# A sliding-window attention block in float16 pairs: other slots in the first three blocks and the last, and 24 low halves made by GpSimd

## The chip, the cores and the metric

One core of a Trainium2 chip runs the whole kernel. The metric is the device time of one execution in microseconds (us); the time before is the median of three runs, 1381.35 us (1379.68 to 1383.4). The engines are named as in the profile: PE (TensorE, with PEld for its weight loads), DVE (VectorE), ACT (ScalarE), POOL (GpSimd) and SP (SyncE, which issues most transfers). Each runs its own instructions in one fixed order and waits on semaphores for the others.

## The reference, cut to what matters

Of the reference's trunk only one layer runs (DEPTH is 1): 4096 tokens, 1024 channels, 16 query heads on 4 key heads, a window of 128 keys, a bias by distance, and one learned sink for each head.

```python
xn = rms_norm(x, norm_g[layer])
q, k, v, z = jnp.split(xn @ w_in, [nq, nq + nkv, nq + 2 * nkv], axis=-1)
o = banded_attention(q_heads(q, B, T), kv_heads(k, B, T), kv_heads(v, B, T),
                     t5_table, SWA_WINDOW, sinks)
y = (merge_heads(o, B, T) * jax.nn.silu(z)) @ w_out
x = x + y
return rms_norm(x, final_g)
```

## The kernel before, in words

**Number format.** Every large operand is held as two float16 tiles: a high half, the value rounded (made by ACT), and a low half, the rest (value minus high half, made by DVE, in `split`, `sum_to` and the functions that return a `low`). A product is three passes: high by high, high by low, low by high.

**Blocks.** The 4096 tokens are worked in 16 blocks of 256 (`block`, the index is `tb`). In each, q, z (the gate) and the output projection o are products of 2 by 2 blocks of the weights with 2 by 2 blocks of the tokens. From block 2 on for q and block 3 on for z and o, they are made with seven products in place of eight, which need sums and differences of the weights' blocks (`LEFT` and `RIGHT` name them: 11, s1 to s4, t1 to t4 ...). Before that (`PLAIN`), and for o in the last block, eight plain products are used. PE time of one product is 48 matmuls for q and z and 12 longer ones for o.

**Preparing the weights.** z's plain weights are split by `plain_z` in four steps, one for each of the blocks 11, 12, 21, 22, in the slots `ZBLOCKS`; block 22 is split by POOL. o's are split by `plain_o` in `OBLOCKS`. The sums are made by `sums`, in chunks of a quarter of the rows (c = 0 to 3), in the slots `SUMS` for q, z and o: one load of 1 MB into the tile `stage` (of which there is one, so that a chunk can only be loaded when the one before is done), a scaling by ACT (L225), four sums or differences by POOL (L187), and for each of the four a split in `sum_to`: high half by ACT (L237), low half by DVE (L239), and a store to DRAM, which is issued from ACT's queue one slot later. The weights are then streamed back from DRAM by SP: `load_s` (L344) into the four `ws` buffers, `load_q` (L361) and `load_fifth` (L356).

**What sets the order.** Each block's steps stand in slots, 25 to a block (`STEADY`, `FIRST`, `NEXT_TO_LAST`, `LAST`); inside a slot in the order of `PHASES`. A step is put there with `at`, or with `at_split` as two parts: high in the phase "high", low in the phase "low". Attention is done in four pairs a block (two groups of heads by two tiles of 128 tokens; `Pair`): scores on PE, `post` and `normalise` on DVE, `exps` on ACT, `turn` (transposes on PE, high half on ACT, low half and mask on DVE: L631, L632), `values` on PE, `gate` on DVE. The slots of the eleven steps come from "pairs"; `PAIRS_BY` moves those of the first three blocks, `SHORT` is the pattern of a pair in the last block. In the slots from `STATIC` = 90 on, PE, ACT, DVE and POOL keep the program's order as it is written. In slots 20 to 89 the builder chooses every engine's order itself from the priorities and its own estimate of times, and in slots 0 to 19 that of all engines but PE. SP's order is always the builder's.

```python
    ZBLOCKS = (6, 7, 9, 11)
    SUMS = {"q": (16, 20, 26, 33), "z": (39, 48, 51, 58), "o": (62, 71, 76, 81)}
    w = work.tile([P, 2, 512], F16, tag="wsp", name="wsp", bufs=3)
    SHORT = (0, 1, 2, 3, 5, 2, 3, 4, 5, 7, 8, 9)
    with tc.manual_schedule(engines={mybir.EngineType.PE}):
        emit(range(20))
    emit(range(20, STATIC))
    with tc.manual_schedule(engines=ENGINES):
        emit(range(STATIC, total))
```

Of the kernel before, what the change touches and what calls it, by code (L numbers as in the profile page):

```python
# [21 lines left out]
P = 128  # L22
# [36 lines left out]
def tile_swa_block(ctx, tc, x, xt, t5, norm_g, final_g, w_q, w_kv, w_z, sinks, w_out, hot, out):  # L59
# [80 lines left out]
    ZBLOCKS = (6, 7, 9, 11)  # L140
    OBLOCKS = (18, 20, 25, 28)
    PAIRS_BY = {0: (1, 4, 2, 3), 1: (2, 2, 2, 2), 2: (0, 1, 0, 2)}
    QSUMS_IN, FIFTH_IN, SPREAD_IN, XLOAD = 7, 9, 5, 7
    SUMS = {"q": (16, 20, 26, 33), "z": (39, 48, 51, 58), "o": (62, 71, 76, 81)}
# [90 lines left out]
    def sum_to(s, where, c, f, scale):  # L235
        w = work.tile([P, 2, 512], F16, tag="wsp", name="wsp", bufs=3)
        nc.scalar.activation(w[:, 0], f, AF.Copy, scale=scale)  # L237
        at("turn", s + 1, lambda: store(where, w, c))
        return lambda: nc.vector.scalar_tensor_tensor(w[:, 1], f, scale, w[:, 0], op0=OP.mult, op1=OP.subtract)  # L239

    def sum_q(s, n, name, c, f):
        return sum_to(s, wqs[n], c, f, 1.0)

    def sum_z(s, n, name, c, f):
        return sum_to(s, wzs[name], c, f, 1.0)
# [303 lines left out]
    class Pair:  # L549


        def __init__(self, tb, gp, t):
            self.tb, self.gp, self.t = tb, gp, t
            self.first = tb == 0 and t == 0
            self.s, self.pt, self.pm, self.c = {}, {}, {}, None

# [20 lines left out]
        def post(self, e):  # L577

            g = 2 * self.gp + e
# [25 lines left out]
        def exps(self, e):  # L605

            for u in range(4 * e, 4 * e + 4):
# [4 lines left out]
        def normalise(self, e):  # L612
            rl = work.tile([P, 4], F32, tag="rl", name="rl", bufs=3)
            nc.vector.reciprocal(rl, self.l[:, 4 * e:4 * e + 4])
            cu = self.c[:, 4 * e:4 * e + 4, :P]
            nc.vector.tensor_tensor(cu, cu, rl[:, :, None].to_broadcast([P, 4, P]), op=OP.mult)  # L616

        def turn(self, e):

            p = ps("tp", 2)  # L620
# [61 lines left out]
    def split_y(tb, name):  # L682

        s = Y[(tb, *YSUM[name][0])] if name in YSUM else Y[tb, int(name[0]) - 1, int(name[1]) - 1]
        YO[name] = work.tile([P, 2, 512], F16, tag="op", name="yo", bufs=4)
        yo = YO[name]
# [3 lines left out]
    def product_o(left, right, p, fresh):  # L690
        k = 0
        for c in range(4):
            for wi, yi in PASSES:
                nc.tensor.matmul(p, YO[left][:, yi, c * P:(c + 1) * P], right(c, wi), start=fresh and k == 0,  # L694
# [163 lines left out]
    SHORT = (0, 1, 2, 3, 5, 2, 3, 4, 5, 7, 8, 9)  # L858

    def moved(pairs, by):  # L860
# [14 lines left out]
    def block(tb):  # L875
# [48 lines left out]
        if isplain["o"]:  # L924
# [3 lines left out]
            for b, s in S["yplain"].items():  # L928
                at_split(s, split_y, tb, b)
            plain(slots, ("o", tb), "bacb" if last else "cbac" if tb + 1 < PLAIN["z"] else "cabc",  # L930
                  lambda i, j, k, p, fresh: product_o(f"{i}{k}", stream(("o", 4 * i + 2 * j + k - 7), f"{k}{j}"), p,
# [160 lines left out]
```

## Time and profile before

| what | before |
|---|---|
| time, median of three runs | 1381.35 us (1379.68 to 1383.4) |
| the profiled execution's own time | 1378.16 us |
| its span, first to last instruction | 1376.4 us |
| PE busy | 1337.0 us, 97% |
| DVE busy | 1199.3 us, 87% |
| ACT busy | 798.6 us, 58% |
| POOL busy | 443.8 us, 32% |

The profile is of one execution. Times are in us from the first instruction, unless marked ns; L239 is line 239 of the kernel. A busy time is the time in which at least one instruction of the engine ran. In brackets behind an instruction stands how long its engine was idle before it, and what ended that.

### The profile page before, as it was taken

The page shows a single profiled execution, that of the slowest core. Times are in us where ns is not written, and L with a number is a line of the kernel's source. Part 1 is how long each engine was busy: PE and PEld are TensorE (multiplying, and loading weights), DVE is VectorE, ACT ScalarE, POOL GpSimd, SP SyncE. Part 2 cuts the span into 40 slices and gives each one's busy share as a digit, 9 for nine tenths or more (in the row PEclk, how much of TensorE's full clock was granted, in tenths as well). Part 3 has the DMA queues.
Part 4 walks back from the last instruction along what each step waited for, and adds up shares of the span by engine and source line. Part 5 has one row for each costly group of instructions (what it writes and reads, how often), then busy time and mean ns, then how long its engine had stood idle before and what let it go on. Part 6 is the DMA issues. An engine that isn't in the chain of part 4 may idle for free.

```text
span 1376.4 us, 39292 instructions
## 1 busy us (share of the span) xinstructions
PE 1337.0 (97%) x16246; PEld 1083.8 (79%) x16246; DVE 1199.3 (87%) x2719; ACT 798.6 (58%) x2052; POOL 443.8 (32%) x406
## 2 busy tenths in 40 slices
PE   5899999999999999999999999999999999999987
PEld 4898678697796978879787887978879687887953
DVE  6989888978889899897989989898898989989895
ACT  6777665655555555555566556556555556655552
POOL 1612432525224143232414224241422424232121
PEclk9999999999999999999999999999999999999999
DMA  9996996889977694866859487694957769495566
GB/s 356 328 374 223 352 390 227 342 321 355 346 276 294 211 342 169 319 242 236 322 184 340 182 301 266 228 340 157 336 213 274 267 230 344 150 335 211 209 236 260
DMA packets 75603, 381.65 MB, mean 277 GB/s; under 512 B 9472, under 2 KB 10784, under 8 KB 42912
## 3 DMA queue, kind: packets, MB, share of 16 engines
q1 hardware_dynamic: 64352, 358.12, 70.6%
q10 hardware_dynamic: 11072, 21.02, 4.1%
q8 instruction: 127, 2.08, 0.6%
q14 instruction: 52, 0.43, 0.1%
HBM read 340.05 MB, written 39.06 MB: 275 GB/s over the span
## 4 chain that ended last, share of the span: by engine, by line
PE 78%; DVE 11%; ACT 4%; issue 3%; DMA 2%; POOL 0%; ACTq 0%; SPq 0%; POOLq 0%; DVEq 0%
PE pa L375 16%; PE pb L375 15%; PE pc L694 11%; PE o L651 6%; PE pa L694 5%; PE s L574 5%; PE pc L375 5%; PE pc L473 5%; PE pb L394 5%; PE tp L624 3%; PE pb L694 3%; DVE wsp L239 2%; DVE c L601 1%; DVE q L427 1%; DVE pt L631 1%
## 5 line engine op out<-in xcount | busy, mean ns | idle before, releaser
L375 PEld LDWEIGHTS <-ws 128*128 128x128 f16 x7008 | 399.3, 98 | 28.2 <-issue 15.9
L694 PEld LDWEIGHTS <-yo 128*128 128x128 f16 x1392 | 134.2, 98 | 144.4 <-issue 2.3
L375 PEld LDWEIGHTS <-wq 128*128 128x128 f16 x3984 | 226.8, 98 | 9.8 <-issue 5.8
L609 ACT ACTIVATE c<-c,m 128x129 f32<-128x129 f32 x512 | 198.9, 391 | 31.8 <-DVE m L601 31.2
L694 PE MATMUL pc<-ws,yo 128*128 128x512 f16 x744 | 170.4, 379 | 0.1
L601 DVE CUSTOM_DVE_ANT_0 c<-s,bias,sink 128x128 f32<-128x128 f32 x496 | 153.2, 349 | 7.8 <-DVE s L592 0.5
L284 POOL TENSOR_TENSOR rr<-ms,mhalf 128x1 f32<-128x1 f32 x62 | 35.6, 582 | 333.6 <-DVE ms L282 267.0
L616 DVE TENSOR_TENSOR c<-c,rl 128x512 f32<-128x512 f32 x128 | 128.0, 1002 | 3.8
L631 DVE SCALAR_TENSOR_TENSOR pt<-tp,pt 128x512 f16<-128x512 f32 x128 | 87.1, 683 | 36.0 <-ACT pt L628 35.9
L574 PE MATMUL s<-K,q 128*128 128x192 f16 x1024 | 107.8, 247 | 3.6 <-DVE m L601 3.3
L688 DVE TENSOR_TENSOR yo<-y,yo 128x512 f16<-128x512 f32 x100 | 82.3, 823 | 33.2 <-ACT yo L687 33.2
L375 PE MATMUL pb<-xs,ws 128*128 128x128 f16 x1872 | 111.2, 219 | 0.0
L322 POOL TENSOR_TENSOR xf<-xf 128x512 f32<-128x512 f32 x56 | 83.9, 1507 | 81.3 <-DVE xb L311 70.5
L404 ACT ACTIVATE mc<-pa 128x512 f32<-128x512 f32 x67 | 39.9, 595 | 117.0 <-PE pa L375 78.3
L404 ACT ACTIVATE mc<-pb 128x512 f32<-128x512 f32 x53 | 31.6, 597 | 129.7 <-PE pb L375 97.0
L375 PE MATMUL pb<-xb,ws 128*128 128x128 f16 x1776 | 106.4, 219 | 0.0
L187 POOL TENSOR_TENSOR wst<-wst 128x512 f32<-128x512 f32 x48 | 71.4, 1497 | 91.2 <-ACT wst L225 49.8
L632 DVE TENSOR_TENSOR pm<-pt,own_m 128x1024 f16<-128x1024 f16 x128 | 96.8, 758 | 3.7
L628 ACT ACTIVATE pt<-tp 128x512 f16<-128x512 f32 x128 | 74.1, 593 | 44.0 <-PE tp L624 39.9
L574 PEld LDWEIGHTS <-q 128*128 128x128 f16 x1024 | 85.9, 98 | 16.7 <-DVE m L601 5.6
L680 POOL TENSOR_TENSOR y<-y,y 128x512 f32<-128x512 f32 x48 | 75.4, 1570 | 68.2 <-DVE y L658 48.8
L609 ACT ACTIVATION_READ_ACCUMULATOR c<-c,m 128x1 f32 x512 | 96.4, 188 | 0.0
(135 smaller groups left out, 2677.6 us busy)
## 6 DMA issues: line engine op xcount, KB each, us to landing
ws<-wos SPq DMA_DIRECT2D x68, 1024.0 KB, 6.0
ws<-wzss SPq DMA_DIRECT2D x52, 1024.0 KB, 6.2
ws<-wost SPq DMA_DIRECT2D x48, 1024.0 KB, 5.5
ws<-wzs SPq DMA_DIRECT2D x47, 1024.0 KB, 5.5
ws<-wqs SPq DMA_DIRECT2D x31, 1024.0 KB, 5.1
xin<-in_x SPq DMA_DIRECT2D x34, 512.0 KB, 4.4
xf<-in_xt SPq DMA_DIRECT2D x32, 512.0 KB, 4.5
r<-in_x SPq DMA_DIRECT2D x30, 512.0 KB, 6.0
```

Source lines behind the costliest of these rows:

```text
L322: nc.gpsimd.tensor_tensor(dst, l, r, op=OP.subtract)
L375: nc.tensor.matmul(place(p, c), left(kc, wi)[:, c * P:(c + 1) * P], right_x(tb, right, kc, xi), start=fresh and c == 0 and k == 0, stop=c ...
L574: nc.tensor.matmul(s[:, hp, 0:3 * HD], lhs, rhs, start=hl == 0, stop=hl == 1)
L601: nc.vector.tensor_tensor_reduce(out=cu, in0=sv, in1=b, scale=-1.0 / SCORE, scalar=sink[:, g, r, hp:hp + 1], op0=OP.add, op1=OP.min, accum ...
L609: nc.scalar.activation(cu, cu, AF.Exp, bias=self.m[:, u:u + 1], scale=-1.0, accum_out=self.l[:, u:u + 1])
L616: nc.vector.tensor_tensor(cu, cu, rl[:, :, None].to_broadcast([P, 4, P]), op=OP.mult)
L631: nc.vector.scalar_tensor_tensor(w[:, 1], p, SP, w[:, 0], op0=OP.mult, op1=OP.subtract)
L632: nc.vector.tensor_tensor(m.rearrange("p l (h q) -> p (l h) q", h=4), w.rearrange("p l (h q) -> p (l h) q", h=4), own_m[:, None, :].to_bro ...
L651: nc.tensor.matmul(o[e * HD:(e + 1) * HD, :], v[:, vt, vi, g * HD:(g + 1) * HD], w[e][:, pi], start=k == 0, stop=k == n - 1)
L680: nc.gpsimd.tensor_tensor(Y[(tb, *dst)], Y[(tb, *l)], Y[(tb, *r)], op=op)
L688: return lambda: nc.vector.tensor_tensor(yo[:, 1], s, yo[:, 0], op=OP.subtract)
L694: nc.tensor.matmul(p, YO[left][:, yi, c * P:(c + 1) * P], right(c, wi), start=fresh and k == 0, stop=k == 11, skip_group_check=not fresh)
```

## The change

- The low halves of q's sums in all four chunks and of z's in chunks 0 and 1 (16 + 8 = 24 of 48) are made by POOL as a plain difference, not by DVE as a scaled one (the scale is 1.0); their store is issued one slot later.
- Other numbers for `ZBLOCKS`, `OBLOCKS`, `PAIRS_BY`, `QSUMS_IN`, `FIFTH_IN`, `SPREAD_IN` (which nothing uses), `XLOAD` and `SUMS`.
- In the last block other slots for the pairs (`SHORT`), for v's differences (`vd`, `dv`), for three steps of z, for the eight products of o and for three of the splits of y. `yo` is kept under a name with the block in it.
- A branch that would scale the probabilities on ACT is added; it is taken for blocks under `SCALED_ON_ACT`, which is 0. `step` is a test while the program is built.

```diff
-    ZBLOCKS = (6, 7, 9, 11)
-    OBLOCKS = (18, 20, 25, 28)
-    PAIRS_BY = {0: (1, 4, 2, 3), 1: (2, 2, 2, 2), 2: (0, 1, 0, 2)}
-    QSUMS_IN, FIFTH_IN, SPREAD_IN, XLOAD = 7, 9, 5, 7
-    SUMS = {"q": (16, 20, 26, 33), "z": (39, 48, 51, 58), "o": (62, 71, 76, 81)}
+    SCALED_ON_ACT = 0
+    LOW_ON_POOL = 6
+    ZBLOCKS = (7, 9, 2, 3)
+    OBLOCKS = (16, 16, 24, 33)
+    PAIRS_BY = {0: (1, 4, 2, 3), 1: (2, 2, 2, 1), 2: (3, 1, 0, 2)}
+    QSUMS_IN, FIFTH_IN, SPREAD_IN, XLOAD = 5, 12, 8, 6
+    SUMS = {"q": (14, 19, 25, 38), "z": (41, 52, 53, 55), "o": (60, 69, 73, 76)}
...
-    def sum_to(s, where, c, f, scale):
+    def sum_to(s, where, c, f, scale, pool=False):
         w = work.tile([P, 2, 512], F16, tag="wsp", name="wsp", bufs=3)
         nc.scalar.activation(w[:, 0], f, AF.Copy, scale=scale)
-        at("turn", s + 1, lambda: store(where, w, c))
+        at("turn", s + (2 if pool else 1), lambda: store(where, w, c))
+        if pool:
+            return lambda: nc.gpsimd.tensor_tensor(w[:, 1], f, w[:, 0], op=OP.subtract)
         return lambda: nc.vector.scalar_tensor_tensor(w[:, 1], f, scale, w[:, 0], op0=OP.mult, op1=OP.subtract)
 
     def sum_q(s, n, name, c, f):
-        return sum_to(s, wqs[n], c, f, 1.0)
+        return sum_to(s, wqs[n], c, f, 1.0, c < LOW_ON_POOL)
 
     def sum_z(s, n, name, c, f):
-        return sum_to(s, wzs[name], c, f, 1.0)
+        return sum_to(s, wzs[name], c, f, 1.0, c + 4 < LOW_ON_POOL)
...
         def normalise(self, e):
+            self.step(e, 2)
             rl = work.tile([P, 4], F32, tag="rl", name="rl", bufs=3)
             nc.vector.reciprocal(rl, self.l[:, 4 * e:4 * e + 4])
+            if self.tb < SCALED_ON_ACT:
...
-        YO[name] = work.tile([P, 2, 512], F16, tag="op", name="yo", bufs=4)
-        yo = YO[name]
+        YO[tb, name] = work.tile([P, 2, 512], F16, tag="op", name="yo", bufs=4)
+        yo = YO[tb, name]
...
-    SHORT = (0, 1, 2, 3, 5, 2, 3, 4, 5, 7, 8, 9)
+    SHORT = (1, 2, 2, 4, 6, 2, 3, 3, 5, 7, 8, 9)
...
-    LAST = dict(STEADY, vd=13, dv=15, zs12=18, zp22=19, zs22=20,
-                pairs={p: tuple(s + d for d in SHORT) for p, s in zip(STEADY["pairs"], (11, 14, 17, 20))},
-                oplain=(24, 27, 26, 28, 29, 32, 30, 33), yplain={"11": 21, "12": 24, "21": 27, "22": 30}, res=25)
+    LAST_PAIRS = (11, 14, 17, 20)
+    LAST_V, LAST_DV, LAST_Z12, LAST_ZP, LAST_Z22 = 17, 18, 19, 21, 23
+    LAST_O = (24, 30, 26, 30, 34, 35, 31, 35)
+    LAST_Y = (21, 24, 27, 29)
+    LAST = dict(STEADY, vd=LAST_V, dv=LAST_DV, zs12=LAST_Z12, zp22=LAST_ZP, zs22=LAST_Z22,
+                pairs={p: tuple(s + d for d in SHORT) for p, s in zip(STEADY["pairs"], LAST_PAIRS)},
+                oplain=LAST_O, yplain=dict(zip(BLOCKS, LAST_Y)), res=25)
```

## Rows read from the trace of the kernel before

**Rows 1.** Page, part 1: busy us, share of the span and instructions.

```profile
PE 1337.0 (97%) x16246; PEld 1083.8 (79%) x16246; DVE 1199.3 (87%) x2719; ACT 798.6 (58%) x2052; POOL 443.8 (32%) x406
```

**Rows 2.** Windows: length; busy PE, PEld, DVE, ACT, POOL; PE's granted clock; DMA share, GB/s.

```profile
50.00:62.00 12.00, 7.57 (x82) 7.16 (x80) 11.51 (x18) 7.03 (x11) 10.15 (x9) 0.72 0.84 272
62.00:230.00 168.00, 162.36 (x2167) 139.45 (x2164) 147.38 (x373) 110.55 (x279) 50.35 (x47) 1.00 0.83 313
...
400.00:725.00 325.00, 325.00 (x3996) 265.82 (x3994) 290.72 (x653) 187.13 (x498) 104.56 (x96) 1.00 0.72 260
...
1290.00:1335.00 45.00, 40.95 (x466) 30.89 (x464) 38.72 (x111) 25.70 (x80) 12.56 (x12) 1.00 0.72 257
...
54.45:61.25 6.80, 5.50 (x48) 5.43 (x49) 6.64 (x8) 2.09 (x4) 6.80 (x6) 0.50 0.76 263
```

**Rows 3.** Waits of PE, 62 to 400 us: total, times, longest.

```profile
PE o L651 <- DVE pt L631: 3.9, 4, 2.3
PE s L574 <- DVE m L601: 2.9, 5, 1.1
PE o L651 <- DVE pm L632: 1.5, 2, 1.2
```

**Rows 4.** Instructions of PE in order of time, at the waits of the first blocks.

```profile
53.24 0.79 PE L375 MATMUL pa<-xb,ws 128*128 128x128 f16 x11 [2.71 <-DVE q L427]
55.75 4.13 PE L375 MATMUL pa<-xb,ws 128*128 128x128 f16 x37 [1.72 <-DVE ws L163]
...
144.30 0.38 PE L651 MATMUL o<-pt,v 128*64 128x512 f16 x1 [2.31 <-DVE pt L631]
...
232.44 0.38 PE L651 MATMUL o<-pt,v 128*64 128x512 f16 x1 [0.86 <-DVE pt L631]
...
333.57 0.51 PE L574 MATMUL s<-K,q 128*128 128x192 f16 x4 [1.14 <-DVE m L601]
```

**Rows 5.** Low halves of sums on DVE, 62 to 236 us: by line.

```profile
L239 DVE SCALAR_TENSOR_TENSOR wsp<-wst,wsp 128x512 f16<-128x512 f32 x23 | 22.4, 983 | 0.5 <-ACT wsp L237 0.5
```

**Rows 6.** Durations by line, whole span: count, ns min/median/max, first and last start.

```profile
L168 POOL TENSOR_TENSOR ws<-wst,ws x4: 1149/1602/1608, 43.5 to 57.8; 128x512 f16<-128x512 f32 x4
L239 DVE SCALAR_TENSOR_TENSOR wsp<-wst,wsp x48: 661/688/1780, 59.8 to 362.5; 128x512 f16<-128x512 f32 x48
L631 DVE SCALAR_TENSOR_TENSOR pt<-tp,pt x128: 652/683/692, 88.1 to 1351.8; 128x512 f16<-128x512 f32 x128
```

**Rows 7.** The normalisations on DVE, 62 to 230 us: count, busy, mean ns.

```profile
L616 DVE TENSOR_TENSOR c<-c,rl 128x512 f32<-128x512 f32 x16 | 12.1, 764 | 0.1
```

**Rows 8.** DVE's instructions of z's weights, in order of time.

```profile
54.64 3.74 DVE L163 SCALAR_TENSOR_TENSOR ws<-wst,gs,ws 128x512 f16<-128x512 f32 x3
```

**Rows 9.** The last block in order of time, DVE and PE.

```profile
1312.60 0.29 DVE L592 COPY_PREDICATED s<-sel,s 128x128 f32<-128x128 int32 x1
...
1314.46 2.08 DVE L514 SCALAR_TENSOR_TENSOR z<-z,cc 128x512 f32<-128x512 f32 x2
...
1316.46 0.68 DVE L631 SCALAR_TENSOR_TENSOR pt<-tp,pt 128x512 f16<-128x512 f32 x1
...
1352.17 2.75 PE L694 MATMUL pb<-ws,yo 128*128 128x512 f16 x12
...
1352.50 0.69 DVE L632 TENSOR_TENSOR pm<-pt,own_m 128x1024 f16<-128x1024 f16 x1
```

**Rows 10.** Waits of PE, 1290 us to the end: total, times, longest.

```profile
PE o L651 <- DVE pt L631: 2.7, 2, 1.8
PE o L651 <- DVE pm L632: 0.9, 2, 0.5
```

**Rows 11.** q's summed weights: the reloads, and PE's first product on them.

```profile
170.47 3.42 SPq L361 DMA_DIRECT2D wq<-wqs x2
...
184.31 2.84 PE L375 MATMUL pb<-xs,wq 128*128 128x128 f16 x48
```

**Rows 12.** The two reloads of rows 11: time to landing.

```profile
DMA to landing us min/median/max: 8.1/8.2/8.3
```

More of the change, by code (lines that the diff above doesn't have):

```diff
@@ L555, in __init__, with step @@
             self.s, self.pt, self.pm, self.c = {}, {}, {}, None
+            self.steps = [0, 0]
+        def step(self, e, n):
+            assert self.steps[e] == n, (self.tb, self.gp, self.t, e, n)
+            self.steps[e] = n + 1
         def scores(self, e):
@@ L577, in post @@
         def post(self, e):
+            self.step(e, 0)
             g = 2 * self.gp + e
@@ L605, in exps @@
         def exps(self, e):
+            self.step(e, 1)
             for u in range(4 * e, 4 * e + 4):
@@ L612, in normalise @@
         def normalise(self, e):
+            self.step(e, 2)
             rl = work.tile([P, 4], F32, tag="rl", name="rl", bufs=3)
             nc.vector.reciprocal(rl, self.l[:, 4 * e:4 * e + 4])
+            if self.tb < SCALED_ON_ACT:
+                for u in range(4):
+                    cu = self.c[:, 4 * e + u, :P]
+                    nc.scalar.activation(cu, cu, AF.Copy, scale=rl[:, u:u + 1])
+                return
             cu = self.c[:, 4 * e:4 * e + 4, :P]
@@ L618, in turn @@
         def turn(self, e):
+            self.step(e, 3)
             p = ps("tp", 2)
@@ L684, in split_y, with product_o @@
         s = Y[(tb, *YSUM[name][0])] if name in YSUM else Y[tb, int(name[0]) - 1, int(name[1]) - 1]
-        YO[name] = work.tile([P, 2, 512], F16, tag="op", name="yo", bufs=4)
-        yo = YO[name]
+        YO[tb, name] = work.tile([P, 2, 512], F16, tag="op", name="yo", bufs=4)
+        yo = YO[tb, name]
         nc.scalar.activation(yo[:, 0], s, AF.Copy)
         return lambda: nc.vector.tensor_tensor(yo[:, 1], s, yo[:, 0], op=OP.subtract)
-    def product_o(left, right, p, fresh):
+    def product_o(tb, left, right, p, fresh):
         k = 0
@@ L693, in product_o @@
             for wi, yi in PASSES:
-                nc.tensor.matmul(p, YO[left][:, yi, c * P:(c + 1) * P], right(c, wi), start=fresh and k == 0,
+                nc.tensor.matmul(p, YO[tb, left][:, yi, c * P:(c + 1) * P], right(c, wi), start=fresh and k == 0,
                                  stop=k == 11, skip_group_check=not fresh)
@@ L930, in block @@
             plain(slots, ("o", tb), "bacb" if last else "cbac" if tb + 1 < PLAIN["z"] else "cabc",
-                  lambda i, j, k, p, fresh: product_o(f"{i}{k}", stream(("o", 4 * i + 2 * j + k - 7), f"{k}{j}"), p,
+                  lambda i, j, k, p, fresh: product_o(tb, f"{i}{k}", stream(("o", 4 * i + 2 * j + k - 7), f"{k}{j}"), p,
                                                       fresh),
@@ L947, in block @@
                      lambda p: add_p(tb, 1, 0, p)]
-            chain(S["o"], ("o", tb), "cab", lambda n, p: product_o(LEFT[n], stream("o", RIGHT[n]), p, n in (0, 1, 3)),
+            chain(S["o"], ("o", tb), "cab", lambda n, p: product_o(tb, LEFT[n], stream("o", RIGHT[n]), p, n in (0, 1, 3)),
                   steps, False)
```

## The prediction, made before the change was run

> **What bounds the kernel now.** I began with busy times by engine: PE is busy for 97% of the span [rows 1], so what can be won without taking products away is what PE waits. Where that is, the windows show [rows 2]: in the 325 us from 400 us on PE is busy in every microsecond, and the code's count for a steady block (14 products of 48 matmuls, 7 of 12, and some 240 others, together about 998) says that the 3996 matmuls there are four blocks, so a block is 81.25 us and a slot 3.25 us. The change touches nothing that runs there but what is left over from the start. PE has idle time in the first three blocks and in the last: 4.4 of 12 us from 50 to 62 us, 5.6 of 168 us from 62 to 230 us, 4.1 of 45 us from 1290 to 1335 us. Next I asked who ends these waits. From 62 to 400 us all three large ones end with DVE, 8.3 us together [rows 3]; in the last block two do, 3.6 us [rows 10]. DVE is busy for 147 of the 168 us, GpSimd for 50 [rows 2]. So the kernel is bound by PE, and in the stretches that are changed by DVE's order: PE stands while DVE does something less urgent first. At 144.30 PE waits 2.31 us and at 232.44 again 0.86 us for the low half of the probabilities (L631) [rows 4]; L239 and the splits of o's weights stand among DVE's work there.
>
> **Part 1: 24 low halves to GpSimd.** In the stretch that matters DVE makes 23 of them in 22.4 us, 0.98 us each [rows 5]; the 24th is the first, at 59.8 us [rows 6]. DVE loses 22.4 + 0.98 = 23.4 us of work. On GpSimd the same difference with the same shape and types is L168, 1.60 us by the median [rows 6]; 24 of them are 38.4 us, which brings GpSimd from 50 to about 89 of 168 us, 53%. It stays off the path as long as the store a slot later is not missed.
>
> What this costs DVE again must be bounded. L239 takes 0.69 us by the median and up to 1.78 us, while L631, whose source lies in PSUM, never takes over 0.69 [rows 6]. So beside GpSimd's work an instruction with two SBUF sources can take 1.09 us more and one with a PSUM source nothing. If each subtraction met one such instruction, DVE would lose 24 x 1.09 = 26.2 us, more than it is given. The lower end is the normalisations in this very stretch, whose mean is 0.764 us [rows 7], 0.08 above L239's median of the same size, although GpSimd was busy for 50 us: 16 x 0.08 = 1.2 us. I take the lower end, since it is measured where the subtractions will lie, so that DVE gains some 22 us in this stretch.
>
> The Trainium skill has a rule against this part (SBUF — State Buffer, section on the two separate sides): GpSimd and a VectorE instruction with two SBUF inputs lock the pair of ports they share for a whole instruction, and the other stands still. By that rule alone the full 38.4 us would be lost where DVE has such an instruction ready. The trace shows it for the lengthened L239, and shows as well that L631 is not touched.
>
> What is it worth to PE? The waits at 144.30 and 232.44 go, 3.2 us. Of the other 5.1 us of [rows 3] I take a third, 1.7 us: one of them, 1.14 us at 333.57 [rows 4], lies beside sums of o, which stay on DVE, and the rest behind other work of DVE. **Minus 4.9 us**; the ends are 0 and minus 8.3.
>
> Queues: the stores are issued by ACT and wait for GpSimd, and behind them stand ACT's exponentials and high halves of the probabilities; one extra slot is 3.25 us, two subtractions. On GpSimd the square root for x's norm (L284) and x's own sums (L322) stand behind the subtractions. The rival for slower has the price.
>
> **Part 2: other slots up to 89.** ZBLOCKS now asks for block 21 first, then 22, then 11 and 12, but PE begins with 11. At 55.75 PE waits 1.72 us for the low half of the last quarter of 11 [rows 4], the first of three such instructions that took 3.74 us [rows 8]. With that of 21 ahead of it the wait grows by a third of that, **plus 1.25 us**. The wait of 2.71 us before (for a q evacuation on DVE) I leave as it is, and also the clock, which was granted at half (1.2 of 2.4 GHz) from 54.45 to 61.25 us [rows 2]: it fell after the first of the two waits, while PE stood in the second. Bounds: both waits and the half clock go (rival 2), or 2.5 us more. The other slots (SUMS, OBLOCKS, PAIRS_BY, QSUMS_IN, FIFTH_IN, XLOAD) I cost at nothing: the order is the builder's there, the chunks of sums follow one another through the single stage buffer, and each transfer lands while PE has products of other matrices to do. If that cover is gone, rival 3 gives the price.
>
> **Part 3: the last block**, where the order is as written. At slot 19 the first pair's values wait 1.79 us for L631 and 0.45 for the mask; at slot 22 the second pair's wait the rest of the 3.6 us [rows 10]. Before the L631 at 1316.46 stand, in slot 18, the post of the third pair's first half, from 1312.60 to 1314.46 = 1.86 us, and the last of two z steps, half of 2.08 us [rows 9]. SHORT moves that post to slot 19 and zs12 moves to 19: 2.9 us less ahead of it. The normalisation that comes one slot later returns up to 0.7 us. So about 0.2 us of this wait is left. For the second pair the same post (of the fourth pair) leaves slot 21, and z's step in 20 goes to 23: its wait goes too. Against this, the last pair's values now have one product of o between the transposes and them where they had two: the mask ran from 1352.50 to 1353.19 while the first of those products had ended by 1352.17, when the second began [rows 9]; that is 0.7 us to wait, with PE's first six matmuls as a small cover. Sum: -3.6 + 0.2 + 0.7 = **minus 2.7 us**; ends 0 and -3.6. The products of o that move behind the values are the same in number, and the tail of additions, norm and stores behind the last product is unchanged. The weights for the last two have three products in between, about 7.8 us by the length in [rows 9] less overlap, to land. The key `YO[tb, name]`, `step` and the branch under SCALED_ON_ACT issue nothing.
>
> **Sum.** -4.9 + 1.25 - 2.7 = -6.35 us. The profiled execution took 1378.16 us, 3.19 us below the median, so 1371.8 us by its own time, and 1375.0 us against the median of 1381.35. A measurement of this kernel can tell about 0.3% from no change, 4.1 us.
>
> **Rivals.**
> 1. *DVE is given nothing.* Every subtraction meets an instruction with two SBUF sources: 26.2 us lost for 23.4 won. The lengthened L239 speaks for it, the normalisations' mean against it. PE's waits of [rows 3] stay: 1378.16 + 1.25 - 2.7 = 1376.7, or 1379.9 us against the median. This is also what would come out if the builder's order hardly followed the new slots. The skill's rule of the port pair leads here.
> 2. *The opening's waits go.* With block 21 and the POOLED block 22 out of the way early, DVE reaches q's evacuation and 11 in time: 2.71 + 1.72 us and half of the 6.8 us of half clock, 3.4 us, go, and the 1.25 is not paid: 1371.8 - 9.1 = 1362.7, or 1365.9 us. For it: DVE had 11.5 of 12 us of work there [rows 2]. Against it: the last quarter of z's raw weights arrives late whatever the order is.
> 3. *Slower: q's summed weights come late.* The reload of the first starts at 170.47 us and takes 8.2 us [rows 11, 12], so it lands at 178.7, and PE uses it at 184.31: 5.6 us of slack. The fourth chunk's slot goes from 33 to 38; if its load really moved by the 5 slots, 16.25 us, PE would stand for 10.6 us in block 2, with nothing behind it to do in order. With half of part 1's gain: 1378.16 + 10.6 + 1.25 - 2.7 - 2.45 = 1384.9, or 1388.1 us. It decides from a delay of 5.6 us on, and makes the kernel slower by 0.3% from about 13.6 us. Against it: chunks follow the stage buffer more than their slot.
>
> **How the numbers follow.** The forecast has 0.45, rival 1 0.18, rival 2 0.2, rival 3 0.17. The forecast's own range, 1370 to 1380, has about a tenth of its weight over 1377.2, where it can't be told from no change. Faster by over 0.3%: 0.4 + 0.2 = 0.6; within: 0.18 + 0.05 = 0.23; slower: 0.17. The range for 8 in 10 goes from 1363, at which rival 2 has a little more than it asks, to 1387, short of rival 3's full price.
>
> **What would show it.** Right: L239 only 24 times, 24 subtractions of about 1.6 us on GpSimd, DVE's busy time from 62 to 230 us down by some 20 us; no wait of PE over 1 us behind L631 before 250 us; PE idle from 1290 to 1335 us about 1.5 us in place of 4.1. Wrong: normalisations or masks at 1.5 us by the mean (rival 1); full clock from 50 to 62 us (rival 2); PE waiting for DMA or idle before the first product on the reloaded weights (rival 3); or an idle time in the last block that only moved from the first pairs to the last.

## The result, and the profile after

| what | before | after |
|---|---|---|
| time, median | 1381.76 us (1379.37 to 1383.4) | 1391.66 us (1388.89 to 1393.79), six runs |
| ratio, 95% interval | | 1.0079 [1.0068, 1.0089] |
| span of the profiled execution | 1376.4 us | 1389.2 us |
| mean clock granted to PE | 0.996 | 0.989 |

The change makes the kernel slower, by about 10 us by the medians and 12.8 us by the two profiled spans. The forecast was 1375.0, its range 1363 to 1387: wrong in sign, and outside the range. The lines of the code have moved by 2 to 19: what was L239 (DVE's low half of a sum) is L243, GpSimd's new one is L242; L163 is L165, L173 L175 (load of a chunk), L187 L189, L344 L348, L375 L379, L574 L584, L601 L612, L616 L634, L631 L650, L632 L651, L651 L670, L688 L707, L694 L713.

Part 1 of the page after, in the columns of [rows 1]:

```profile
PE 1342.9 (97%) x16246; PEld 1086.9 (78%) x16246; DVE 1192.8 (86%) x2695; ACT 799.4 (58%) x2052; POOL 464.9 (33%) x430
```

PE has the same 16246 matmuls but is busy for 5.9 us longer, and its idle time, span less busy, is 46.3 us where it was 39.4. These two, 5.9 + 6.9, are the whole 12.8 us. DVE is busy for 6.5 us less over the span, and that has bought nothing. The windows say where, in the columns of [rows 2]:

```profile
50.00:62.00 12.00, 6.01 (x73) 5.69 (x71) 10.01 (x15) 8.48 (x13) 8.71 (x9) 0.75 0.98 319
62.00:230.00 168.00, 159.23 (x2061) 134.48 (x2060) 136.04 (x336) 104.92 (x259) 71.84 (x66) 0.98 0.82 311
230.00:400.00 170.00, 161.99 (x1878) 126.59 (x1876) 136.26 (x314) 89.69 (x231) 61.77 (x52) 0.96 0.82 309
...
1303.00:1348.00 45.00, 43.21 (x512) 33.84 (x510) 39.41 (x114) 27.16 (x84) 12.10 (x12) 1.00 0.76 270
...
400.00:1303.00 903.00, 903.00 (x11096) 738.72 (x11095) 808.57 (x1808) 519.67 (x1379) 290.87 (x267) 1.00 0.72 258
```

The window of the kernel before that [rows 2] does not show:

```profile
230.00:400.00 170.00, 166.35 (x1945) 130.70 (x1943) 143.29 (x329) 94.58 (x234) 64.50 (x52) 1.00 0.87 331
```

PE idles for 6.0 us in the first stretch (4.4 before), 8.8 in the second (5.6 before) and 8.0 in the third (3.7 before). The steady blocks have no idle time, as before. The last block, which now comes 13 us later, idles for 1.8 us where [rows 2] gives 4.1: that part did what its sum forecast. The clock column is the other half of the loss: 0.98 and 0.96 where it was 1.00. Waits of PE from 62 to 400 us, to be laid beside [rows 3]:

```profile
PE s L584 <- DVE m L612: 6.6, 1, 6.6
PE pb L713 <- DMA ws<-wos: 3.6, 1, 3.6
PE pa L713 <- DMA ws<-wos: 2.4, 1, 2.4
PE o L670 <- DVE pm L651: 2.0, 1, 2.0
```

The many waits of before have made room for four large ones. Behind a low half of the probabilities (3.9 us in four waits of [rows 3]) PE now waits for 0.2 us. So the waits that the prediction wanted gone are gone, and larger ones stand at other places. Those rows of PE, in order of time:

```profile
53.97 0.77 PE L379 MATMUL pa<-xb,ws 128*128 128x128 f16 x11 [2.58 <-ACT ws L164]
58.15 4.13 PE L379 MATMUL pa<-xb,ws 128*128 128x128 f16 x37 [3.41 <-DVE ws L165]
...
160.88 0.82 PE L584 MATMUL s<-K,q 128*128 128x192 f16 x4 [6.62 <-DVE m L612]
...
265.34 5.28 PE L713 MATMUL pb<-ws,yo 128*128 128x512 f16 x12 [3.60 <-DMA ws<-wos]
...
335.45 1.01 PE L670 MATMUL o<-pm,dv 128*64 128x512 f16 x5 [1.99 <-DVE pm L651]
...
355.34 4.27 PE L713 MATMUL pa<-ws,yo 128*128 128x512 f16 x12 [2.42 <-DMA ws<-wos]
```

**The longest, 6.62 us.** Scores wait until DVE has read the ones before them (L612). DVE's row of work ahead of that, in order of time:

```profile
152.31 2.52 DVE L707 TENSOR_TENSOR yo<-y,yo 128x512 f16<-128x512 f32 x2
154.76 0.17 DVE L627 RECIPROCAL rl<-l 128x4 f32<-128x4 f32 x1
154.96 1.55 DVE L634 TENSOR_TENSOR c<-c,rl 128x512 f32<-128x512 f32 x1
156.44 1.75 DVE L707 TENSOR_TENSOR yo<-y,yo 128x512 f16<-128x512 f32 x1
158.11 0.48 DVE L603 COPY_PREDICATED s<-sel,s 128x128 f32<-128x128 int32 x2
158.50 1.78 DVE L315 TENSOR_TENSOR xb<-xf,xb 128x1024 f16<-128x1024 f32 x1
160.20 0.34 DVE L612 CUSTOM_DVE_ANT_0 c<-s,bias,sink 128x128 f32<-128x128 f32 x1
```

The low halves of y and of x stand ahead of the scores that PE waits for, and beside GpSimd's work one of them takes 1.75 us where a low half of that size takes 0.68.

**The two waits for a transfer.** Rows of SP's queue after: first instruction's start, time until the last one was issued, line, tile, count.

```profile
236.86 1.24 SPq L175 DMA_DIRECT2D wst<-in_wz  x2
239.77 9.60 SPq L348 DMA_DIRECT2D ws<-wos  x2
257.40 0.81 SPq L175 DMA_DIRECT2D wst<-in_wz  x2
258.31 2.25 SPq L348 DMA_DIRECT2D ws<-wos  x4
```

The same queue in the kernel before:

```profile
234.81 1.35 SPq L173 DMA_DIRECT2D wst<-in_wz  x2
243.94 9.37 SPq L344 DMA_DIRECT2D ws<-wos  x4
256.78 0.81 SPq L173 DMA_DIRECT2D wst<-in_wz  x2
257.68 1.25 SPq L344 DMA_DIRECT2D ws<-wos  x2
```

Before, four loads of o's weights are issued ahead of the load of z's last chunk; after, two, and the next stands behind it. That load waits for the single stage buffer, in the waits of SP's queue from 240 to 270 us:

```profile
SPq L175 <- DVE wsp L243: 8.0, 1, 8.0
```

So for 8.0 us a load that PE needs soon is queued behind one that can't start, and PE then stands for 3.6 us at 265.34. The wait at 355.34 has the same shape, at o's last chunk: two loads of o's weights are issued between o's third and fourth chunk, where the kernel before issues five.

**The clock.** Within or just behind each of these waits PE's clock was granted at half, 1.2 of 2.4 GHz. Up to PE's last product the kernel before has one such stretch, that of the opening [rows 2]; the changed kernel has five:

```profile
56.00:62.90 6.90, 4.75 (x43) 4.69 (x44) 4.14 (x5) 3.34 (x6) 5.23 (x5) 0.51 0.94 334
158.40:165.30 6.90, 4.42 (x13) 1.94 (x14) 6.90 (x15) 4.18 (x12) 6.02 (x5) 0.51 0.93 384
264.25:271.10 6.85, 5.76 (x17) 2.35 (x17) 6.70 (x16) 4.75 (x9) 5.05 (x5) 0.50 1.00 423
335.90:339.30 3.40, 3.40 (x31) 2.91 (x29) 3.31 (x5) 2.91 (x11) 0.63 (x1) 0.50 0.82 330
356.40:359.80 3.40, 3.40 (x10) 1.50 (x9) 3.40 (x4) 2.97 (x11) 3.32 (x3) 0.50 1.02 429
```

PE is busy for 21.7 us in these five, and for 5.5 us in the one of before. Half of the 16.2 us between, 8.1 us, is an estimate of the most that the clock can have added; the page's 5.9 us more of busy PE is what the whole span shows.

### The profile page after: what moved, and what is told of

Read it like the earlier page. It is cut to its first block, busy times and chain, and to the rows that moved or that the text cites. A ratio compares the mean times of both kernels' runs of the same rounds, so it can differ in the third digit from the quotient of the medians.

```text
span 1389.2 us, 39298 instructions
## 1 busy us (share of the span) xinstructions
PE 1342.9 (97%) x16246; PEld 1086.9 (78%) x16246; DVE 1192.8 (86%) x2695; ACT 799.4 (58%) x2052; POOL 464.9 (33%) x430
## 4 chain that ended last, share of the span: by engine, by line
PE 77%; DMA 3%; DVE 1%; ACT 0%; POOL 0%; issue 0%; SPq 0%; POOLq 0%; ACTq 0%
PE pa L379 15%; PE pb L379 15%; PE pc L713 10%; PE pa L713 6%; PE o L670 6%; PE s L584 5%; PE pb L398 5%; PE pc L379 5%; PE pc L477 5%; PE pb L713 4%; PE tp L643 3%; DMA ws<-wos 1%; DMA wst<-in_wz 1%; DMA wst<-in_wo 0%; DMA wzss<-wsp 0%; DVE pm L651 0%
## 5 line engine op out<-in xcount | busy, mean ns | idle before, releaser
L379 PEld LDWEIGHTS <-ws 128*128 128x128 f16 x7008 | 400.3, 98 | 25.0 <-issue 14.4
L713 PEld LDWEIGHTS <-yo 128*128 128x128 f16 x1392 | 135.3, 99 | 154.2 <-issue 15.3
L379 PEld LDWEIGHTS <-wq 128*128 128x128 f16 x3984 | 227.0, 98 | 9.1 <-issue 4.9
L713 PE MATMUL pc<-ws,yo 128*128 128x512 f16 x744 | 172.3, 382 | 0.0
L612 DVE CUSTOM_DVE_ANT_0 c<-s,bias,sink 128x128 f32<-128x128 f32 x496 | 153.5, 349 | 7.5 <-PE tp L643 0.2
L634 DVE TENSOR_TENSOR c<-c,rl 128x512 f32<-128x512 f32 x128 | 134.1, 1050 | 3.8
L650 DVE SCALAR_TENSOR_TENSOR pt<-tp,pt 128x512 f16<-128x512 f32 x128 | 87.4, 684 | 37.3 <-ACT pt L647 37.2
L584 PE MATMUL s<-K,q 128*128 128x192 f16 x1024 | 107.6, 247 | 6.6 <-DVE m L612 6.6
L707 DVE TENSOR_TENSOR yo<-y,yo 128x512 f16<-128x512 f32 x100 | 85.1, 852 | 32.1 <-ACT yo L706 32.1
L379 PE MATMUL pb<-xs,ws 128*128 128x128 f16 x1872 | 111.2, 219 | 0.0
L379 PE MATMUL pb<-xb,ws 128*128 128x128 f16 x1776 | 105.5, 219 | 0.2 <-DVE z L518 0.2
L584 PEld LDWEIGHTS <-q 128*128 128x128 f16 x1024 | 86.6, 99 | 20.1 <-DVE m L612 7.5
L651 DVE TENSOR_TENSOR pm<-pt,own_m 128x1024 f16<-128x1024 f16 x128 | 98.2, 769 | 4.3 <-PE o L670 0.6
L189 POOL TENSOR_TENSOR wst<-wst 128x512 f32<-128x512 f32 x48 | 69.3, 1455 | 79.4 <-ACT wst L227 60.7
```

Of the source, the lines that this page charges most:

```text
L379: nc.tensor.matmul(place(p, c), left(kc, wi)[:, c * P:(c + 1) * P], right_x(tb, right, kc, xi), start=fresh and c == 0 and k == 0, stop=c ...
L584: nc.tensor.matmul(s[:, hp, 0:3 * HD], lhs, rhs, start=hl == 0, stop=hl == 1)
L612: nc.vector.tensor_tensor_reduce(out=cu, in0=sv, in1=b, scale=-1.0 / SCORE, scalar=sink[:, g, r, hp:hp + 1], op0=OP.add, op1=OP.min, accum ...
L650: nc.vector.scalar_tensor_tensor(w[:, 1], p, SP, w[:, 0], op0=OP.mult, op1=OP.subtract)
L651: nc.vector.tensor_tensor(m.rearrange("p l (h q) -> p (l h) q", h=4), w.rearrange("p l (h q) -> p (l h) q", h=4), own_m[:, None, :].to_bro ...
L707: return lambda: nc.vector.tensor_tensor(yo[:, 1], s, yo[:, 0], op=OP.subtract)
```

## The experiments

The theories, as the expectations name them. Theory D: what costs is the other order that the builder gives to slots 20 to 89 once the low halves stand elsewhere. Theory C: it is the work on GpSimd itself, its length in a chunk and what it takes from DVE. The first four runs speak of theories A (the new slots cost) and B (the subtractions cost); two later ones (S and L) are explained in their expectations. The diffs are cut and stand against the changed kernel, that of e18 against e1; where the text says that slots are as before, they are put back too. The ratio is that to the kernel before on the same chip, whose median lay between 1380.1 and 1381.2 us in every batch.

### One part at a time

**e1_last_only**: of the change only the last block's new slots.

```diff
-    LOW_ON_POOL = 6
-    ZBLOCKS = (7, 9, 2, 3)
+    LOW_ON_POOL = 0
+    ZBLOCKS = (6, 7, 9, 11)
...
```

> Only the last block has its new slots; the first three blocks and all 48 low halves are as before. In the changed kernel PE's excess over its own pace from 1300 us on is 2.8 us where it was 6.0. Theory A (the slots up to 89 make the builder put the wrong work ahead) and theory B (the 24 subtractions on GpSimd cost more than they give) both say: 3 us faster than before, about 1378 to 1379 us, and PE idle in the last 90 us about 3 us less. If it is not faster, the last block gave nothing and the loss in front was smaller than 13 us.

Measured: 1375.88 us, ratio 0.9975 [0.9961, 0.9989]. This version beats both kernels.

**e2_low_only**: only the 24 low halves on GpSimd, with their store a slot later; all slots as before.

```diff
     LOW_ON_POOL = 6
-    ZBLOCKS = (7, 9, 2, 3)
+    ZBLOCKS = (6, 7, 9, 11)
...
-    SHORT = (1, 2, 2, 4, 6, 2, 3, 3, 5, 7, 8, 9)
+    SHORT = (0, 1, 2, 3, 5, 2, 3, 4, 5, 7, 8, 9)
...
```

> Only the 24 low halves go to GpSimd (with the later store); every slot is as before. Theory A: not slower than before, 1375 to 1382 us, with no wait of PE on a transfer over 1 us. Theory B: 1388 us or more, with PE waiting for DVE's masks, posts or low halves for 6 us or more beyond those of before.

Measured: 1392.02 us, ratio 1.0088 [1.0073, 1.0104]: the whole loss by itself.

**e3_slots_only**: all the new slots, the low halves on DVE.

```diff
-    LOW_ON_POOL = 6
+    LOW_ON_POOL = 0
```

> All new slots, but all 48 low halves stay on DVE. Theory A: slow as the changed kernel or worse, 1387 to 1398 us, since the order of chunks and loads is the new one and DVE has its 23 us back. Theory B: 1375 to 1380 us, the 3 us of the last block below before.

Measured: 1378.01 us, ratio 0.9986 [0.9976, 0.9995]. Against e1 the new slots of the first blocks cost 0.0011, some 2 us, though the two intervals overlap. So theory A falls, and theory B's times came out in e2 and e3.

**e4_old_sums**: the changed kernel with the old `SUMS`.

```diff
-    SUMS = {"q": (14, 19, 25, 38), "z": (41, 52, 53, 55), "o": (60, 69, 73, 76)}
+    SUMS = {"q": (16, 20, 26, 33), "z": (39, 48, 51, 58), "o": (62, 71, 76, 81)}
```

> The changed kernel, but with the slots of before for the chunks of sums (SUMS). Theory A in the form that SUMS are the slots that matter (a chunk's load stands ahead of streamed weights in SyncE's queue and waits for the single stage buffer): the waits on ws<-wos at 265 and 355 us go, with the half clock behind them, some 10 us, so 1378 to 1384 us. If other slots matter (ZBLOCKS, OBLOCKS, PAIRS_BY): 1388 us or more. Theory B: 1388 us or more.

Measured: 1390.94 us, ratio 1.008 [1.0065, 1.0095], like the changed kernel. In its trace PE, DVE, ACT, GpSimd and the transfers that SP issues stand in the changed kernel's order, instruction by instruction. So the new slots of the chunks are not it, and rival 3, which put the loss on the fourth chunk's slot, falls.

Where e2 loses is the first clue. Its windows, in the columns of [rows 2], and its subtractions on GpSimd (count, ns min/median/max, first and last start):

```profile
62.00:230.00 168.00, 162.66 (x2155) 139.85 (x2153) 137.26 (x353) 110.88 (x279) 75.40 (x68) 0.99 0.82 314
230.00:400.00 170.00, 155.43 (x1813) 120.62 (x1811) 140.00 (x299) 87.16 (x221) 63.78 (x53) 1.00 0.84 312
```

```profile
L242 POOL TENSOR_TENSOR wsp<-wst,wsp x24: 1149/1248/2137, 59.4 to 232.2; 128x512 f16<-128x512 f32 x24
```

Up to 230 us, where all of the 24 subtractions but two begin, PE idles for 5.3 us, no more than in the kernel before (5.6). Behind it, from 230 to 400 us, it idles for 14.6 us, where that had 3.7. These 10.9 us are nearly all of the 12.4 us between the two spans (1388.8 and 1376.4), and they lie where next to no moved work is left. That speaks against any theory in which the moved work is itself in PE's way.

### Which low halves, and how much work

Each of these has the last block's new slots and all the others as before.

**e7_low_q**: q's 16 on GpSimd, z's 8 on DVE.

```diff
-    LOW_ON_POOL = 6
+    LOW_ON_POOL = 4
```

> As the run with only the new last block, with the 16 low halves of q's sums on GpSimd and z's on DVE. If each moved low half costs the same, 12 us x 16/24 = 8 us: 1384 us. If the loss comes where q's chunks meet the first products (before 180 us): 1387 us. If it comes from z's chunks, which lie just ahead of the stretch from 230 to 400 us in which most of the loss was seen: 1374 to 1378 us.

Measured: 1388.21 us, ratio 1.006 [1.0036, 1.0083].

**e8_low_z**: z's 8 on GpSimd, q's 16 on DVE.

```diff
-        return sum_to(s, wqs[n], c, f, 1.0, c < LOW_ON_POOL)
+        return sum_to(s, wqs[n], c, f, 1.0, False)
```

> As the run with only the new last block, with the 8 low halves of z's sums in two chunks on GpSimd and q's on DVE. Same cost for each: 1380 us. Loss from q: 1374 to 1377 us. Loss from z: 1386 to 1388 us.

Measured: 1378.0 us, ratio 0.9981 [0.9969, 0.9994], within the intervals the same as e1. The loss comes with q's.

**e5_no_low**: the 24 low halves are not made at all; DRAM gets the high half twice, so the low parts of q's and of half of z's summed weights are missing from the result.

```diff
-            return lambda: nc.gpsimd.tensor_tensor(w[:, 1], f, w[:, 0], op=OP.subtract)
+            return lambda: None
...
-        at("turn", s + (2 if pool else 1), lambda: store(where, w, c))
+        at("turn", s + (2 if pool else 1), lambda: store(where, w[:, 0:1].to_broadcast([P, 2, 512]) if pool else w, c))
```

> As the run with only the new last block (1375.9 us), but the 24 low halves in question are left out: neither DVE nor GpSimd makes them, and the high half is stored in their place, so the q and z weights of these chunks lack their low parts. Theory C (DVE's 23 us are worth something, and GpSimd's 38 us beside DVE take it back and more): 1366 to 1372 us. Theory D (the builder orders the first three blocks anew as soon as DVE has 23 us less to do, and that order is the loss): 1380 us or more.

Measured: 1381.67 us, ratio 1.0004 [0.9994, 1.0014]. With 24 instructions less on DVE and none more on GpSimd the kernel is 0.0029, some 4 us, slower than e1: less work, another order, more time.

**e6_both**: each of the 24 is made by DVE and then once more by GpSimd in the same place.

```diff
-            return lambda: nc.gpsimd.tensor_tensor(w[:, 1], f, w[:, 0], op=OP.subtract)
+            def both():
+                nc.vector.scalar_tensor_tensor(w[:, 1], f, scale, w[:, 0], op0=OP.mult, op1=OP.subtract)
+                nc.gpsimd.tensor_tensor(w[:, 1], f, w[:, 0], op=OP.subtract)
+            return both
```

> As the run with only the new last block, but each of the 24 low halves is made twice: by DVE as before, and then by GpSimd into the same place. DVE is not relieved and GpSimd has the 38 us. Theory C: 1388 to 1400 us, GpSimd's work alone costs 12 us or more. Theory D: under 1384 us, since DVE's work, and with it the order, stays about what it was.

Measured: 1387.73 us, ratio 1.0053 [1.0034, 1.0071], between the two theories' ranges. It was meant to give GpSimd's part without DVE's relief, but it changes the order and a chunk's length as well, so by itself it tells neither theory from the other.

### The order as it is written

Here the written order begins earlier. Each pair differs by where the 24 are made; SP's order, and in the first pair all orders up to slot 59, are still the builder's.

**e9_s60_dve** and **e10_s60_pool**: `STATIC` at 60, the low halves on DVE and on GpSimd.

```diff
-    STATIC = 90
+    STATIC = 60
```

> New last block, all low halves on DVE, but the order of PE, ACT, DVE and POOL is as written from slot 60 on (STATIC = 60 in place of 90). This is the reference for the next run; between 1370 and 1395 us, unknown which, since the written order of blocks 2 and 3 has not been seen.

> The run before it with the 24 low halves on GpSimd. Theory D (most of the 12 us is the builder's other order in slots 60 to 89, after the moved work): at most 4 us slower than its partner, and PE's excess from 225 to 400 us, which was 19 us with the builder's order against 7.4 with the low halves on DVE, within 3 us of its partner's. Theory C (GpSimd's work itself): 8 us slower or more.

Measured: 1422.5 us, ratio 1.031 [1.0292, 1.0329], and 1421.98 us, 1.0311 [1.0287, 1.0334].

**e11_s20_dve** and **e12_s20_pool**: `STATIC` at 20; with the low halves on GpSimd the store stands one slot after the split.

```diff
-    STATIC = 90
+    STATIC = 20
...
-        at("turn", s + (2 if pool else 1), lambda: store(where, w, c))
+        at("turn", s + 1, lambda: store(where, w, c))
```

> New last block, all low halves on DVE, the order as written from slot 20 on. The reference for the next run; 1375 to 1420 us, since the written order of the first blocks has not been seen.

> The run before it with the 24 low halves on GpSimd, and their store in the slot after the high half as for DVE. With the order fixed nothing can be ordered anew. Theory D: from 5 us faster to 2 us slower than its partner. Theory C: 8 us slower or more, with DVE's instructions that have two SBUF sources longer in the mean.

Measured: 1455.46 us, ratio 1.0551 [1.0533, 1.0568], and 1455.61 us, 1.0547 [1.0531, 1.0563]. In the written order the move is worth nothing that these intervals show, neither a loss nor a gain. But these kernels are 40 and 75 us slower than the others, with one wait of 28.5 and of 27.0 us in the first pair, and such waits could hide a loss of 12 us. The test needed was the builder's own orders, held fixed.

### Order and engine apart

Every instruction that the program emits has the same number in two kernels that differ only in the engine of the 24. So the order that the builder chose for one can be written down and given to the other, as edges between neighbours on an engine, without a semaphore:

```diff
+    made = {i.name: i for i in nc.cur_bb.bb.instructions}
+    after = mybir.DependencyInfo(mybir.DependencyClass.NoSync, mybir.DependencyReason.DATA)
...
+                        tc.add_manual_dep(i, last.name, after, reason="order kept")
```

All engines, SP among them, then run in the kept order to the last instruction, and the traces show it so; each moved low half stands where it was dispatched.

**e13_order_of_e1**: e1's order, the 24 on GpSimd, their store one slot after the split as in e1.

> The 24 low halves are on GpSimd (store a slot later, as before the change), everything else is as in the kernel with the last block's slots alone (1375.9 us), and every engine keeps exactly the order that the builder chose for that kernel; each low half stands in GpSimd's order where it was dispatched in VectorE's. Theory D (what costs is the other order that the builder chooses when it sees the low halves on GpSimd): 1370 to 1378 us. Theory C (what costs is the work on GpSimd itself, its length in the chunk and beside VectorE): 1384 to 1391 us.

Measured: 1381.23 us, ratio 0.9996 [0.9987, 1.0005]: between the ranges of the two theories.

**e14_own_order**: the same program, ordered anew by the builder; the store is, as in e13, one slot after the split.

```diff
-        at("turn", s + (2 if pool else 1), lambda: store(where, w, c))
+        at("turn", s + 1, lambda: store(where, w, c))
```

> The same program, but the builder orders it anew with the 24 low halves on GpSimd; it is the other row of the table. Both theories: 1386 to 1391 us, since the order is new and the work is on GpSimd; at 1378 or less the loss would have come from the store's slot.

Measured: 1377.64 us, ratio 0.9976 [0.9965, 0.9986]. A miss for both theories, and the most telling run: all 24 subtractions are on GpSimd, and nothing is lost against e1. By its expectation that points at the store's slot, which is taken up below.

**e15_own_order_dve**: e14's order, the 24 on DVE.

> The order that the builder chose for the run before, kept on every engine, but the 24 low halves are made by VectorE again. Theory D: as slow as that run or slower, 1386 to 1395 us. Theory C: 1374 to 1380 us.

Measured: 1379.65 us, ratio 0.9992 [0.9983, 1.0001]. It was to be slow by theory D because e14 was thought to be slow; as e14's order is fast, it tells little between the two.

**e16_after_order_dve**: the changed kernel's order, the 24 on DVE.

> The changed kernel with the order that the builder chose for it kept on every engine, but its 24 low halves made by VectorE, each where it was dispatched. Theory D: as slow as the changed kernel or slower, 1389 to 1400 us. Theory C: 1376 to 1382 us.

Measured: 1394.8 us, ratio 1.0093 [1.0077, 1.0109]: in theory D's range, and well above theory C's.

The ratios as a table:

| order chosen by the builder for | low halves on DVE | on GpSimd |
|---|---|---|
| e1 (they are on DVE) | 0.9975 | 0.9996 |
| e14 (on GpSimd, store as before) | 0.9992 | 0.9976 |
| the changed kernel (on GpSimd) | 1.0093 | 1.0079 |

Read along a row, the engine is worth 0.0014 to 0.0021, some 2 to 3 us, and in favour of the engine that the order was made for. In every row the two intervals overlap, and the slower kernel is also the one with the added edges; none was run with the edges alone, so these 2 to 3 us may not be the engine's. Read down a column, the order is worth 0.0083 to 0.0118, some 11 to 16 us. Theory C as the cause of the loss falls: the changed kernel's order is slow without any of the work on GpSimd, and another order is fast with all of it. At most the 3 us of e13 are left to it.

The trace of e16 shows the changed kernel's waits, at the same steps, without a subtraction on GpSimd. First rows of PE, then SP's queue:

```profile
164.16 0.82 PE L584 MATMUL s<-K,q 128*128 128x192 f16 x4 [3.77 <-DVE m L612]
...
269.52 4.44 PE L713 MATMUL pb<-ws,yo 128*128 128x512 f16 x12 [3.90 <-DMA ws<-wos]
```

```profile
239.86 0.86 SPq L175 DMA_DIRECT2D wst<-in_wz  x2
243.64 9.60 SPq L348 DMA_DIRECT2D ws<-wos  x2
261.03 0.81 SPq L175 DMA_DIRECT2D wst<-in_wz  x2
```

The trace of e14 has SP's order of the kernel before, four loads of o's weights ahead of z's last chunk, and PE idles for 4.8 us in the window that had 8.0. First its window in the columns of [rows 2], then SP's queue:

```profile
230.00:400.00 170.00, 165.22 (x1958) 130.38 (x1956) 142.51 (x321) 94.69 (x233) 66.52 (x56) 1.00 0.86 328
```

```profile
236.45 0.86 SPq L175 DMA_DIRECT2D wst<-in_wz  x2
246.41 9.37 SPq L348 DMA_DIRECT2D ws<-wos  x4
258.91 0.82 SPq L175 DMA_DIRECT2D wst<-in_wz  x2
```

### Is it the store's slot?

e14 differs from the slow kernels also by its store, one slot after the split instead of two.

**e17_after_store1**: the changed kernel with the store one slot after the split.

```diff
-        at("turn", s + (2 if pool else 1), lambda: store(where, w, c))
+        at("turn", s + 1, lambda: store(where, w, c))
```

> The changed kernel with one number back: the store of the 24 sums that have their low half on GpSimd stands one slot after the split, as before the change, not two. Theory S (it is the later slot of the store that spoils the order, by way of the tiles that the sums wait for): 1375 to 1382 us, near the kernel with all new slots and the low halves on VectorE (1378.0). Theory L (any new order may come out well or badly, and the run with the store a slot later came out badly by chance): 1384 to 1393 us.

Measured: 1391.35 us, ratio 1.0073 [1.006, 1.0087].

**e18_e1_store2**: e1 with the store of these 24 two slots after the split, the low halves on DVE.

```diff
-    LOW_ON_POOL = 0
+    LOW_ON_POOL = 6
...
-            return lambda: nc.gpsimd.tensor_tensor(w[:, 1], f, w[:, 0], op=OP.subtract)
+            return lambda: nc.vector.scalar_tensor_tensor(w[:, 1], f, scale, w[:, 0], op0=OP.mult, op1=OP.subtract)
```

> The kernel with the last block's slots alone (1375.9 us), all low halves on VectorE, and only the store of these 24 sums two slots after the split. Theory S: 1384 to 1391 us, as slow as with the low halves on GpSimd. Theory L, and a theory by which the later store costs only together with GpSimd's low halves: 1373 to 1380 us.

Measured: 1377.76 us, ratio 0.9977 [0.9968, 0.9986]. So the slot alone spoils nothing, and taking it out of the changed kernel mends nothing. But neither edit gave the engines another order of work (the stores' own places in ACT's queue apart): in the trace of e17 PE, DVE, ACT, GpSimd and the transfers that SP issues stand in the changed kernel's order, in that of e18 in e1's. So theory L, by which a new order may come out either way, was not tested by these two, and theory S falls for the changed kernel only.

With the old slots it does not fall. Up to the last block e2 and e14 differ by the store's slot alone: 1.0088 and 0.9976. The new last block is 0.0025 of the 0.0112 between them (e1, whose order of PE is that of the kernel before up to the last block). The other 0.0087, some 12 us, comes with the later store when the low halves are on GpSimd. The two kernels have another order on every engine; that this order, and not the later store itself, costs the 12 us was not run with e2's order kept.

**What stays open.** No single number of the change makes the order bad by itself. With the old slots it takes the low halves on GpSimd and the later store together (e2 is slow, e14 and e18 are fast). With the new slots the low halves on GpSimd are enough, with the store in either slot (the changed kernel and e17 are slow, e3 is fast). Why the builder comes to the bad order is not shown. One thing goes with nearly all of these: how many loads of o's weights SP issues between o's third and fourth chunk. It is two in the changed kernel, e2, e4, e7, e16 and e17 (1388 to 1395 us) and five in the kernel before, e1, e3, e8, e13, e14, e15 and e18 (1376 to 1381 us); e6 (1387.7 us) has five too, and loses elsewhere (PE idles for 11.6 us from 62 to 230 us), and e5, which loads o's chunks earlier, has none. That is a sign by which to know most of the slow orders. That SP's order alone is worth those microseconds was not tried, and in e2 most of the waits from 230 to 400 us end with DVE.

## Why the prediction was wrong, step by step

**The bound** was read rightly: PE, its waits in the first three blocks and in the last, and nothing in the steady blocks.

**Part 1 failed, and with it the sign.** The failing step is "The waits at 144.30 and 232.44 go, 3.2 us", and the third of the others with it, together minus 4.9 us. The named waits did go. But the price was taken from a list of waits in which each was removed with all else left in its place, and slots 20 to 89 have no place of their own: the builder orders them anew. In place of minus 4.9 us the new order cost plus 12 us (e2, and e7 against e1). Of the store a slot later the prediction asked only whether it would be missed, not what it does to the order (e2 against e14). The prediction knew that the order is the builder's; it used this only to cost the other slots at nothing. It is the same mistake from the other side: where a planner re-orders, neither "this wait goes" nor "this costs nothing" can be read off the old trace, and the range must hold what another order may cost. The runs here give that size: 1376 to 1392 us for programs with nearly the same work.

In a kept order the move itself is worth between minus 2 and plus 3 us (the table's rows), within the prediction's ends of 0 and minus 8.3 only where it gains.

**The terms inside part 1.** GpSimd's subtraction was put at 1.60 us; it took less. DVE was to gain some 22 of 23.4 us, with 1.2 us lost to GpSimd's work. Count, ns min/median/max, first and last start of the subtractions after, and the normalisations beside them (count, busy, mean ns), to be laid beside [rows 7]:

```profile
L242 POOL TENSOR_TENSOR wsp<-wst,wsp x24: 1147/1163/2135, 59.2 to 235.7; 128x512 f16<-128x512 f32 x24
```

```profile
L634 DVE TENSOR_TENSOR c<-c,rl 128x512 f32<-128x512 f32 x16 | 15.2, 960 | 0.1
```

The normalisations' mean rose from 764 to 960 ns, so the lower bound that the prediction chose for the loss was too low. How much DVE gained shows best in one order with the work on either engine. Part 1 of the page of e16, of which the changed kernel's page above is the counterpart, and DVE's low halves in e16:

```profile
PE 1344.0 (96%) x16246; PEld 1086.6 (78%) x16246; DVE 1204.4 (86%) x2719; ACT 799.1 (57%) x2052; POOL 439.1 (32%) x406
```

```profile
L242 DVE SCALAR_TENSOR_TENSOR wsp<-wst,wsp 128x512 f16<-128x512 f32 x24 | 20.1, 837 | 6.4 <-ACT wsp L239 6.2
```

DVE's busy time falls from 1204.4 to 1192.8 us, 11.6 us, for 20.1 us of work taken away: 8.5 us came back, in the main as longer instructions on DVE. In e14's order it falls by 11.0 us (1200.2 to 1189.2). So DVE kept about half, between the forecast's term (1.2 us lost) and rival 1's (26.2 us lost).

The Trainium skill warns against this kind of move (Perfetto Trace Analysis, section on optimizing Scalar and DVE operations): since the two engines share a port, moving operations from one to the other might not help. Here the trace agrees in part, with half of the relief kept. The Trainium skill's stricter rule, by which the engine that comes second stands still for the whole instruction (SBUF — State Buffer, section on the two separate sides), would have let DVE keep nothing if every subtraction met such an instruction. Where the two meet alone the trace agrees: of two normalisations one takes its usual 0.69 us, and the next, begun 0.20 us into a subtraction, ends 0.55 us behind it:

```profile
75.03 1.30 POOL L242 TENSOR_TENSOR wsp<-wst,wsp 128x512 f16<-128x512 f32 x1 [6.67 <-ACT wsp L239]
75.23 1.65 DVE L634 TENSOR_TENSOR c<-c,rl 128x512 f32<-128x512 f32 x1
```

So what DVE kept, 11.6 us, it kept where a subtraction met no such instruction, or only its end; that is argued from this one place.

**Part 2** was right where it had a number. PE's wait for the last quarter of 11 was to grow by 1.25 us; it grew by 1.69 (3.41 at 58.15, 1.72 in [rows 4]), while the wait before it shrank by 0.13. The mechanism is the forecast one: before, PE went on behind the first of three low halves that DVE began at 54.64; after, behind the second of three begun at 55.27, and that one took 1.75 us. The first blocks' new slots, put at plus 1.25 in all, are worth some 2 us between e3 and e1, and SUMS, put at nothing, are worth nothing that shows (e4).

**Part 3** was right: minus 2.7 us was forecast, e1 measures a ratio of 0.9975, which is minus 3.5 us with an interval from 1.5 to 5.4. By the windows PE's idle time there falls from 4.1 to 1.8 us. Two of its terms were off, in opposite directions. Of the waits of [rows 10] the first pair's, 1.79 us, was to shrink to 0.2; it is still there:

```profile
1332.42 0.59 PE L670 MATMUL o<-pt,v 128*64 128x512 f16 x3 [1.68 <-DVE pt L650]
```

Before that low half DVE now makes v's difference, which the change moved from slot 15 to 18 and the sum left out, and a normalisation that took 1.70 us. The other three waits are gone, and the 0.7 us that the last pair was to wait did not come: the row above is the only wait of PE for DVE from 1303 us to the end.

**The rivals.** Rival 1 is half right in its mechanism and has no part in the loss. Rival 2 did not come: the opening's half clock is there as before. Rival 3 forecast 1388.1, the nearest to the result, for a reason that didn't occur: PE waits nowhere for q's summed weights (none of the waits above is for wq), and e4 with the old slots is just as slow. A right number was no sign of a right reason.

## What to carry to other kernels

Where a builder or planner orders part of a kernel, treat a change there as a new order, and first see from the trace whether it is one: e4, e17 and e18 changed a number, but neither the order of the engines' work nor the time. Read from the trace which work waits ahead of which on each queue, SP's too, and expect the change to move all of it. To learn what an edit is worth by itself, keep the old order and change only the edit, and keep the new order and undo the edit; the table of both says at once whether the work or its order costs. And a relief of an engine that isn't the bound is worth only those waits in which it comes last: DVE lost 6.5 us of busy time here and PE gained none.

## What the runs showed of the hardware that was not expected

The same subtraction took 1.16 us by the median on GpSimd where the nearest row, L168, had 1.60 us, yet single ones took up to 2.14 us. DVE's low halves of the probabilities, whose source lies in PSUM, took at most 0.695 us in all 128 places of the changed kernel, while normalisations of the same size with two sources in SBUF took up to 1.78 us. And a wait could be paid twice: behind the 6.62 us at 160.88 and the 3.60 us at 265.34 PE's clock was granted at half for 6.9 us each, so that by estimate up to half of the busy time in them, 2.2 and 2.9 us, came on top.
